# Neighbourhood attention with both heads of a block kept on the two halves of the 128 rows

## The chip, the cores and the metric

The kernel runs on one NeuronCore of a Trainium2 chip. The metric is the device time of one execution in microseconds, as the median of several runs. The engines are TensorE (PE; its weight loads are listed apart as PEld), VectorE (DVE), ScalarE (ACT), GpSimd (POOL) and SyncE (SP, which issues most of the DMAs).

## What is computed

Two layers of a diffusion backbone work on 256 latent tokens and 256 context tokens of width 1024, all in float32. Each layer projects the tokens once; the columns feed a gated linear attention (GLA, 4 heads) and a neighbourhood attention (8 heads of width 64). Both outputs go through one output projection, and a SwiGLU follows (layer 0) or a mixture of 8 experts (layer 1). The part that matters here is the neighbourhood attention. In outline:

```
s_loc = q . k[clamped grid window of the query] + bias        (latent queries)
s_ctx = q . kc                                                (all context keys)
p     = softmax(concat(s_loc, s_ctx))                         (one softmax, float32)
out   = p_loc . v[window] + p_ctx . vc
context queries: softmax(q . kc / sqrt(64)) . vc              (layer 0 only)
```

The kernel computes the scores of a latent query against all 256 latent and 256 context keys at once; keys outside the window get a bias of -1e30.

## The kernel before

**Precision by splitting.** A float32 product on PE is made of products in `float32r`, the rounded type. A tensor x is split in a rounded part r (an ACT copy that writes `float32r`) and a rest l = x - r (a DVE subtraction), and a product of two split tensors is r.r + r.l + l.r (`mm3`, L209 to L212: three matmuls of 128 contraction rows and up to 512 columns).

**Where heads lie.** `nq` and `nk` hold the projected queries and keys transposed: partition = head dimension, so one block b of 128 partitions holds two heads, head 2b on partitions 0 to 63 and head 2b+1 on 64 to 127. `natt` (L936 to L1042) has four blocks.

**`prep(b)` (L941 to L957)** makes the operands of one block. For each of the two heads (j = 0, 1) it builds a tile K2 of 128 partitions with the rounded keys on the head's own half (ACT, L952) and the rest of the keys on the other half (DVE, L954), a tile Q2 with the rounded queries on the own half (ACT, L953) and the queries cast to `float32r` on the other half (DVE, L955), and a tile ql with the rest of the queries on the own half (DVE, L956) and zeros on the other (POOL, L948, once for each pool). So one matmul over 128 rows, Q2 by K2, sums r.r + r.l (L976), and a second, ql by K2, adds l.r (L977). That is two matmuls a head, four for the two heads of a block, all in the full 128 x 128 form, and two ACT and three DVE instructions a head in `prep`, each on 64 partitions.

**One item** is one head of one block for 128 queries, for latent queries (`ctx` = 0, 512 keys) or context queries (`ctx` = 1, 256 keys). Layer 0 has 32 items, 16 of each; layer 1 has 16 items, latent only. Stages of an item: `n1` takes a PSUM bank, runs L976 and L977, adds the bias on DVE (L981), takes the maximum (DVE, L984) and the exponential with its sum (ACT, L987). `n1b` takes the reciprocal (DVE, L993) and scales (DVE, L994). `n2` transposes the probabilities 128 columns at a time (PE, L1004) and copies them out of PSUM (ACT, L1005). `n3`, once for both heads and 256 queries, multiplies by the values (PE, L1019: 128 rows by 64 columns, the two heads on the two column halves), and `na_done` splits the result into HR (ACT, L1077) and HL (DVE, L1078).

**Order.** `run` (L1023) emits `n1` of item i, `n1b` of item i-1, `n2` of item i-3 and `n3` of item i-4, with two yields for an item. `weave(main, filler, each)` (L217) puts steps of other work in after each yield: with `each` a triple (rate, count, later rate), `rate` steps for each of the first `count` yields and `later rate` after. For `natt` the filler is the r projection with its gate (L928 to L930), the transposes of the GLA output (`o_turn`, L1132 to L1137), and, in layer 0, four adaLN column blocks (L356, loads of `w_ada`). `RATE` (L2037) holds the triple of each layer. Within this part a scheduler that builds the program then orders each engine's instructions by priority, which follows the emission, and by when it reckons that their inputs are ready; the engines run them in that fixed order. `prep(0)` is emitted before `natt` starts, at the end of the GLA core; `prep(1)` after the second item; `prep(b+2)` after the last item of block b, since it writes the same buffers. `bias(b)` loads the bias tile of a block through SP (L965, two buffers).

**After it.** The output projection (L622) starts once the last `na_done` is through. In layer 1 it is followed by the router and the experts, whose weights (about 350 MB) are streamed from HBM to the end of the program; the first of their loads are issued with the output projection.

Of the kernel before, what the change touches and what calls it, by code (L numbers as in the profile page):

```python
# [93 lines left out]
def kernel(ctx: ExitStack, tc: tile.TileContext, A: dict, out: bass.AP):  # L94
    nc = tc.nc
# [183 lines left out]
    ident = B_("ident")  # L279
# [656 lines left out]
    def natt(l, full, C, first, nq, nk, nv, done):  # L936


        parts, lows = {}, {}

        def prep(b):  # L941
            pool = na if b % 2 else first[0].pool
            K2 = [pool.tile([P, NT], F32R, tag=f"K2{j}", bufs=1, name=f"K2{j}") for j in range(2)]
            Q2 = [pool.tile([P, nq.shape[2]], F32R, tag=f"Q2{j}", bufs=1, name=f"Q2{j}") for j in range(2)]
            if pool not in lows:
                lows[pool] = [pool.tile([P, nq.shape[2]], F32R, name=f"ql{j}") for j in range(2)]
                for j in range(2):
                    nc.gpsimd.memset(lows[pool][j][64 - 64 * j:P - 64 * j].bitcast(F32), 0.0)  # L948
            ql = lows[pool]
            for j in range(2):  # L950
                own, other = slice(64 * j, 64 * j + 64), slice(64 - 64 * j, P - 64 * j)
# [7 lines left out]
        items = [dict(b=b, ctx=cx, j=j, qt=qt) for b in range(4) for cx in range(2 if full else 1) for j in range(2) for qt in range(2)]  # L959
        Bt, PTs = {}, {}  # L960
        na = None

        def bias(b):
            t = na.tile([P, 2, 6, 64], F32, tag="B", bufs=2, name="B")
            nc.sync.dma_start(t, relD[l][2 * b:2 * b + 2].rearrange("h r q x c -> (r q) h x c"))  # L965
            Bt[b] = t

        def n1(it):
            b, j, qt, cx = it["b"], it["j"], it["qt"], it["ctx"]
            if cx == 0 and j == 1 and qt == 1 and b < 2:  # L970
                bias(b + 2)
            n = 256 if cx else 512
# [5 lines left out]
            if cx == int(full) and j == 1 and qt == 1 and b < 2:  # L978
                prep(b + 2)
            if not cx:  # L980
                nc.vector.tensor_tensor(out=pS[:, 0:256], in0=pS[:, 0:256],  # L981
                                        in1=Bt[b][:, j, 2 - 2 * qt:6 - 2 * qt, :].rearrange("p x c -> p (x c)"), op=ALU.add)
# [5 lines left out]
            it["p"], it["n"], it["rs"] = pr, n, rs  # L988

        def n1b(it):  # L990
            pr, n, rs = it["p"], it["n"], it["rs"]
# [4 lines left out]
        def n2(it):  # L996
            b, j, qt, cx = it["b"], it["j"], it["qt"], it["ctx"]
            nkb = it["n"] // P
            if qt == 0:
                PTs[b, cx, j] = na.tile([P, 4, 256], F32, tag="PT", bufs=3, name="PT")  # L1000
            PT = PTs[b, cx, j]
            pt = ps()
            for i in range(nkb):
                nc.tensor.transpose(pt[:, i * P:(i + 1) * P], it["p"][:, i * P:(i + 1) * P], ident)  # L1004
            nc.scalar.activation(PT[:, :nkb, qt * P:(qt + 1) * P],  # L1005
                                 pt[:, :it["n"]].rearrange("p (a t) -> p a t", a=nkb), AF.Copy)

        def n3(it):

            b, j, qt, cx = it["b"], it["j"], it["qt"], it["ctx"]  # L1010
            if qt == 0 or j == 0:
                return
            kbs = [2, 3] if cx else [0, 1, 2, 3]
            pts = [PTs.pop((b, cx, jj)) for jj in range(2)]
            bank = ps()
            for i, kb in enumerate(kbs):
                for jj in range(2):
                    h = 2 * b + jj
                    nc.tensor.matmul(bank[64 * jj:64 * jj + 64, 0:256], nv[kb][:, h * 64:(h + 1) * 64], pts[jj][:, i, :],  # L1019
                                     start=i == 0, stop=i == len(kbs) - 1)  # L1020
            done(b, cx, bank)

        def run(na_pool):  # L1023
# [1117 lines left out]
```

## Time and profile before

| | |
|---|---|
| median of 3 runs | 1880.4 us (1879.72 to 1882.68) |
| the profiled execution, its own time | 1879.96 us |
| its span, first to last instruction | 1878.1 us |
| mean granted TensorE clock | 0.984 |
| PE, PEld, DVE, ACT, POOL busy | 1797.8, 1297.5, 1189.9, 922.7, 84.2 us |
| neighbourhood attention, layer 0 | about 213 to 300 us from the span's start |
| neighbourhood attention, layer 1 | about 882 to 934 us |

The span is one execution on the chip as the hardware profiler recorded it; the profiled execution's own time is 1.86 us longer than its span. Each engine runs its own queue in order. A wait is listed with the instruction that waited and the one that ended the wait. The busy time of PE counts a matmul until its modelled end; in a stream of matmuls each one starts before the one ahead of it has ended, so the price of a matmul in a stream is the distance between two starts, not the duration in the row.

### The profile page before, as it was taken

What the parts mean: (1) busy time and instruction counts of PE and PEld (TensorE: products, weight loads), DVE (VectorE), ACT (ScalarE), POOL (GpSimd) and SP (SyncE); (2) the same over time, 40 slices, a digit from 0 to 9 for tenths busy, and PEclk for the clock granted to TensorE, in tenths of its full rate; (3) what the DMA queues carried; (4) which work ended last, traced back from release to release, by engine and by line L of the source; (5) the groups of instructions that cost most, each with busy time, mean ns of one, the idle gap of its engine ahead of it and who ended that gap; (6) DMA issues with size and microseconds to landing.
All of it is one profiled execution on the core that took longest, in us unless ns stands there. A gap on an engine that the chain in (4) does not pass through costs nothing. (4 is left out here: it accounts for less than half of the span.)

```text
span 1878.1 us, 25461 instructions
## 1 busy us (share of the span) xinstructions
PE 1797.8 (96%) x8773; PEld 1297.5 (69%) x8773; DVE 1189.9 (63%) x1750; ACT 922.7 (49%) x1329; POOL 84.2 (4%) x103
## 2 busy tenths in 40 slices
PE   5999899999999998999899999999999999999995
PEld 3688566877788887787577853588886358888731
DVE  4457686478642345368879951599996249999701
ACT  3443376522222336443757831577774247777501
POOL 2100200110000002001000000000000000000000
PEclk8999999999999999999899999999999999999998
DMA  9432546267763332424299999999999999999996
GB/s 327 137 105 52 183 163 221 79 197 255 227 190 92 121 109 66 141 79 130 58 341 340 325 347 404 409 409 404 409 378 350 407 406 408 404 409 385 340 408 262
DMA packets 203321, 491.90 MB, mean 262 GB/s; under 512 B 29744, under 2 KB 71248, under 8 KB 203184
## 3 DMA queue, kind: packets, MB, share of 16 engines
q1 hardware_dynamic: 201152, 483.12, 71.0%
q0 software_dynamic: 2032, 7.08, 1.1%
q8 instruction: 71, 1.16, 0.3%
q14 instruction: 66, 0.54, 0.1%
HBM read 485.94 MB, written 4.98 MB: 261 GB/s over the span
## 5 line engine op out<-in xcount | busy, mean ns | idle before, releaser
L170 DVE TENSOR_TENSOR wl<-raw,wr 128x1024 fp32r<-128x1024 f32 x446 | 536.1, 1225 | 132.9 <-ACT wr L169 128.7
L169 ACT ACTIVATE wr<-raw 128x1024 fp32r<-128x1024 f32 x446 | 465.8, 1059 | 295.3 <-PE ps L211 152.0
L210 PE MATMUL ps<-wr,HR 128*128 128x512 f32 x736 | 299.3, 407 | 2.5 <-ACT wr L169 2.5
L211 PE MATMUL ps<-wl,HR 128*128 128x512 f32 x736 | 294.4, 400 | 7.5 <-DVE wl L170 6.5
L212 PE MATMUL ps<-wr,HL 128*128 128x512 f32 x736 | 292.3, 397 | 0.0
L210 PE MATMUL ps<-HR,wr 128*128 128x512 f32 (+1 forms) x592 | 220.3, 373 | 9.6 <-ACT HR L1979 6.2
L211 PE MATMUL ps<-HL,wr 128*128 128x512 f32 (+1 forms) x592 | 218.5, 369 | 3.4 <-POOL HL L521 1.7
L212 PE MATMUL ps<-HR,wl 128*128 128x512 f32 (+1 forms) x592 | 217.4, 367 | 0.5 <-DVE wl L170 0.5
L211 PEld LDWEIGHTS ps<-wl,HR 128*128 128x128 f32 x736 | 139.5, 190 | 47.0 <-DVE wl L170 14.7
L210 PEld LDWEIGHTS ps<-wr,HR 128*128 128x128 f32 x736 | 139.5, 190 | 40.5 <-issue 4.7
L212 PEld LDWEIGHTS ps<-wr,HL 128*128 128x128 f32 x736 | 139.2, 189 | 32.5
L210 PEld LDWEIGHTS ps<-HR,wr 128*128 128x128 f32 x592 | 111.6, 189 | 41.8 <-issue 8.6
L211 PEld LDWEIGHTS ps<-HL,wr 128*128 128x128 f32 x592 | 112.3, 190 | 23.6 <-DVE HL L1984 3.4
L212 PEld LDWEIGHTS ps<-HR,wl 128*128 128x128 f32 x592 | 112.4, 190 | 19.2 <-DVE wl L170 1.0
L1600 PE MATMUL ps<-raw,xw 128*64 128x512 f32 (+1 forms) x596 | 117.2, 536 | 2.2 <-DMA raw<-in_moe_w_gate 1.1
L1615 DVE TENSOR_TENSOR hid<-hid,ps 128x512 f32<-128x512 f32 (+1 forms) x47 | 31.3, 665 | 132.9 <-PE ps L1600 132.9
L210 PE MATMUL ps<-wr,tr 128*128 128x512 f32 x280 | 111.9, 400 | 0.0
L211 PE MATMUL ps<-wl,tr 128*128 128x512 f32 x280 | 110.6, 395 | 0.0
L212 PE MATMUL ps<-wr,tl 128*128 128x512 f32 x280 | 110.4, 394 | 0.0
L1600 PEld LDWEIGHTS ps<-raw,xw 128*64 128x64 f32 x596 | 40.7, 137 | 66.4 <-issue 53.3
L405 DVE SCALAR_TENSOR_TENSOR sums<-raw,condS,sums 128x512 f32<-128x512 f32 x98 | 71.6, 761 | 19.6 <-DMA raw<-in_w_ada 18.8
L1600 PE MATMUL ps<-raw,tw 128*64 128x512 f32 x272 | 67.2, 605 | 3.9 <-DMA raw<-in_moe_w_down 2.8
(368 smaller groups left out, 2433.6 us busy)
## 6 DMA issues: line engine op xcount, KB each, us to landing
raw<-in_moe_w_down SPq DMA_DIRECT2D x180, 512.0 KB
raw<-in_moe_w_gate SPq DMA_DIRECT2D x169, 512.0 KB
raw<-in_moe_w_up SPq DMA_DIRECT2D x167, 512.0 KB
raw<-in_w_ada SPq DMA_DIRECT2D x80, 512.0 KB
raw<-in_w_in SPq DMA_DIRECT2D x48, 512.0 KB
HR1w<-in_moe_w_up SPq DMA_DIRECT2D x24, 512.0 KB
raw<-in_ffn_w_gate SPq DMA_DIRECT2D x22, 512.0 KB
raw<-in_ffn_w_up SPq DMA_DIRECT2D x22, 512.0 KB
```

Source lines behind the costliest of these rows:

```text
L169: nc.scalar.activation(wr, raw, AF.Copy)
L170: nc.vector.tensor_tensor(out=wl, in0=raw, in1=wr.bitcast(F32), op=ALU.subtract)
L210: nc.tensor.matmul(o, lr, rr, start=start, stop=False)
L211: nc.tensor.matmul(o, lr, rl, start=False, stop=False)
L212: nc.tensor.matmul(o, ll, rr, start=False, stop=stop)
L405: nc.vector.scalar_tensor_tensor(out=o, in0=i_, scalar=s_, in1=o, op0=ALU.mult, op1=ALU.add)
L1600: nc.tensor.matmul(o[a * HALF:(a + 1) * HALF, 0:n], x, raw[:, a * n:(a + 1) * n], start=start, stop=stop)
L1615: nc.vector.tensor_tensor(out=hid, in0=hid, in1=st.pop((fb, 1))[:, 0:w], op=ALU.mult)
```

## The change

A block's two heads stay where the projection put them. `prep(b)` splits the whole 128-partition block at once, keys and queries: one ACT copy and one DVE subtraction for each. An item is now both heads of a block for 128 queries. Its scores are three products for each head (r.r, r.l, l.r) of 64 contraction rows, head 0 on rows 0 to 63 and head 1 on rows 64 to 127, in turns, each head into a PSUM bank of its own. The zeroed halves (L948) and the cast (L955) are gone. `n1`, `n1b`, `n2` become `scores`, `soft`, `scaled`, `turned`, the last three once a head; an item's `turned` and `n3` come one item (two heads) later instead of three and four heads later, with four yields to an item. Layer 1's triple changes from (.65, 40, .65) to (1, 11, .5). The load of the next bias tile is emitted after the last use of its buffer instead of ahead of it.

```diff
         def prep(b):
             pool = na if b % 2 else first[0].pool
-            K2 = [pool.tile([P, NT], F32R, tag=f"K2{j}", bufs=1, name=f"K2{j}") for j in range(2)]
-            Q2 = [pool.tile([P, nq.shape[2]], F32R, tag=f"Q2{j}", bufs=1, name=f"Q2{j}") for j in range(2)]
-            if pool not in lows:
-                lows[pool] = [pool.tile([P, nq.shape[2]], F32R, name=f"ql{j}") for j in range(2)]
-                for j in range(2):
-                    nc.gpsimd.memset(lows[pool][j][64 - 64 * j:P - 64 * j].bitcast(F32), 0.0)
-            ql = lows[pool]
-            for j in range(2):
-                own, other = slice(64 * j, 64 * j + 64), slice(64 - 64 * j, P - 64 * j)
-                nc.scalar.activation(K2[j][own], nk[own, b, :], AF.Copy)
-                nc.scalar.activation(Q2[j][own], nq[own, b, :], AF.Copy)
-                nc.vector.tensor_tensor(out=K2[j][other], in0=nk[own, b, :], in1=K2[j][own].bitcast(F32), op=ALU.subtract)
-                nc.vector.tensor_copy(Q2[j][other], nq[own, b, :])
-                nc.vector.tensor_tensor(out=ql[j][own], in0=nq[own, b, :], in1=Q2[j][own].bitcast(F32), op=ALU.subtract)
-            parts[b] = K2, Q2, ql
+            parts[b] = []
+            for nm, t in (("k", nk), ("q", nq)):
+                hi, lo = (pool.tile([P, t.shape[2]], F32R, tag=nm + x, bufs=1, name=nm + x) for x in "rl")
+                nc.scalar.activation(hi, t[:, b, :], AF.Copy)
+                nc.vector.tensor_tensor(out=lo, in0=t[:, b, :], in1=hi.bitcast(F32), op=ALU.subtract)
+                parts[b] += [hi, lo]
...
-        def n1(it):
...
-            pS = ps()
-            K2, Q2, ql = parts[b]
+        def scores(it):
+            b, qt, cx = it["b"], it["qt"], it["ctx"]
+            n = it["n"] = 256 if cx else 512
+            it["s"] = [ps() for _ in range(2)]
+            kr, kl, qr, ql = parts[b]
             tok = slice(cx * 256 + qt * P, cx * 256 + (qt + 1) * P)
-            nc.tensor.matmul(pS[:, :n], Q2[j][:, tok], K2[j][:, NT - n:NT], start=True, stop=False)
-            nc.tensor.matmul(pS[:, :n], ql[j][:, tok], K2[j][:, NT - n:NT], start=False, stop=True)
+            for i, (q, k) in enumerate(((qr, kr), (qr, kl), (ql, kr))):
+                for j in range(2):
+                    nc.tensor.matmul(it["s"][j][:, :n], q[half[j], tok], k[half[j], NT - n:NT], start=i == 0, stop=i == 2)
...
-            for i in range(n + 4):
-                if i < n:
-                    n1(items[i])
-                if i == 1:
+            for i in range(n + 1):
+                it, old = (items[i] if i < n else None), (items[i - 1] if i else None)
+                if it:
+                    scores(it)
+                    soft(it, 0)
+                if i == 0:
                     prep(1)
                 yield
-                if 0 <= i - 1 < n:
-                    n1b(items[i - 1])
-                if 0 <= i - 3 < n:
-                    n2(items[i - 3])
-                if 0 <= i - 4 < n:
-                    n3(items[i - 4])
+                if it:
+                    soft(it, 1)
+                    if it["ctx"] == 0 and it["qt"] == 1 and it["b"] < 2:
+                        bias(it["b"] + 2)
+                if old:
+                    turned(old, 0)
+                yield
+                if it:
+                    scaled(it, 0)
+                if old:
+                    turned(old, 1)
+                yield
+                if it:
+                    scaled(it, 1)
+                if old:
+                    n3(old)
                 yield
...
-    RATE, FILL = ((1.2, 17, .5), (.65, 40, .65)), (5, 6)
+    RATE, FILL = ((1.2, 17, .5), (1, 11, .5)), (5, 6)
```

## Rows read from the trace of the kernel before

**Rows 1.** Busy by stage: length, PE, PEld, DVE, ACT, POOL, clock, DMA, GB/s.
```profile
213.00:300.00 87.00, 79.04 (x467) 51.67 (x468) 70.38 (x172) 57.50 (x135) 8.72 (x9) 0.98 0.66 220
882.00:934.00 52.00, 42.66 (x217) 30.23 (x218) 45.42 (x107) 35.04 (x75) 1.64 (x3) 0.87 0.29 94
1100.00:1864.00 764.00, 751.88 (x3420) 488.58 (x3420) 485.65 (x498) 415.20 (x475) 2.34 (x3) 1.00 1.00 391
```

**Rows 2.** The same view in stretches of 10 us, inside layer 1's stage.
```profile
890.00:900.00 10.00, 6.33 (x21) 4.60 (x20) 9.72 (x23) 5.33 (x11) 0.00 (x0) 0.66 0.26 73
```

**Rows 3.** Waits of PE in layer 1's stage, 882 to 934: total, times, longest us.
```profile
PE ps L1004 <- DVE p L994: 8.0, 6, 3.7
```

**Rows 4.** Waits of PE in layer 0's stage, 213 to 300.
```profile
PE ps L211 <- DVE wl L170: 3.6, 1, 3.6
PE ps L1004 <- DVE p L994: 3.4, 4, 1.3
```

**Rows 5.** DVE groups by line, 882 to 934: busy us, mean ns, idle before.
```profile
L954 DVE TENSOR_TENSOR K<-nk,K 64x512 fp32r<-64x512 f32 x6 | 4.1, 685 | 0.2
L955 DVE CAST Q<-nq 64x256 fp32r<-64x256 f32 x6 | 3.0, 499 | 0.2
...
L956 DVE TENSOR_TENSOR ql<-nq,Q 64x256 fp32r<-64x256 f32 x6 | 2.5, 417 | 0.1
...
L365 DVE TENSOR_TENSOR adarows<-ps,adarows 128x512 fp32r<-128x512 f32 x1 | 0.7, 693 | 0.0
```

**Rows 6.** DVE groups by line, 213 to 300.
```profile
L954 DVE TENSOR_TENSOR K<-nk,K 64x512 fp32r<-64x512 f32 x6 | 4.3, 714 | 0.2
L956 DVE TENSOR_TENSOR ql<-nq,Q 64x512 fp32r<-64x512 f32 x6 | 4.1, 685 | 0.1
...
L955 DVE CAST Q<-nq 64x512 fp32r<-64x512 f32 x6 | 2.5, 419 | 0.1
```

**Rows 7.** ACT groups by line, 882 to 934.
```profile
L952 ACT ACTIVATE K<-nk 64x512 fp32r<-64x512 f32 x6 | 3.7, 622 | 0.1
...
L953 ACT ACTIVATE Q<-nq 64x256 fp32r<-64x256 f32 x6 | 2.4, 406 | 2.1 <-PE ps L976 2.1
```

**Rows 8.** Timeline of PE around an expert's scatter: start us, us, instruction, count.
```profile
1196.71 0.39 PE L211 MATMUL ps<-wl,HR 128*128 128x512 f32 x1
1196.94 0.40 PE L212 MATMUL ps<-wr,HL 128*128 128x512 f32 x1
1197.27 0.51 PE L1733 MATMUL ps<-yr,GT 64*128 64x512 f32 x2
1197.60 0.41 PE L1734 MATMUL ps<-yl,GT 64*128 64x512 f32 x2
1197.83 0.41 PE L1733 MATMUL ps<-yr,GT 64*128 64x512 f32 x2
1198.07 0.40 PE L1734 MATMUL ps<-yl,GT 64*128 64x512 f32 x2
1198.40 0.50 PE L210 MATMUL ps<-wr,HR 128*128 128x512 f32 x1
1198.74 0.40 PE L211 MATMUL ps<-wl,HR 128*128 128x512 f32 x1
```

**Rows 9.** Timeline of PE at an item of 256 keys in layer 0.
```profile
245.56 0.28 PE L976 MATMUL ps<-K,Q 128*128 128x256 f32 x1
...
245.68 0.28 PE L977 MATMUL ps<-K,ql 128*128 128x256 f32 x1
...
245.79 0.40 PE L210 MATMUL ps<-wr,HR 128*128 128x512 f32 x1
```

**Rows 10.** Waits of SP's queue, 882 to 934.
```profile
SPq L965 <- DVE ps L981: 10.2, 1, 10.2
```

**Rows 11.** Timeline of the end of layer 1's stage.
```profile
929.33 0.48 DVE L994 TENSOR_SCALAR p<-p,ri 128x512 f32<-128x512 f32 x1
...
930.58 3.89 PE L1019 MATMUL ps<-PT,nv 128*64 128x256 f32 x16
...
934.40 0.73 PE L622 MATMUL psh<-wr,HR 128*128 128x512 f32 x2
```

More of the change, by code (lines that the diff above doesn't have):

```diff
@@ L936, in natt @@
     def natt(l, full, C, first, nq, nk, nv, done):
-        parts, lows = {}, {}
+        parts = {}
+        half = [slice(0, 64), slice(64, P)]
         def prep(b):
             pool = na if b % 2 else first[0].pool
-            K2 = [pool.tile([P, NT], F32R, tag=f"K2{j}", bufs=1, name=f"K2{j}") for j in range(2)]
-            Q2 = [pool.tile([P, nq.shape[2]], F32R, tag=f"Q2{j}", bufs=1, name=f"Q2{j}") for j in range(2)]
-            if pool not in lows:
-                lows[pool] = [pool.tile([P, nq.shape[2]], F32R, name=f"ql{j}") for j in range(2)]
-                for j in range(2):
-                    nc.gpsimd.memset(lows[pool][j][64 - 64 * j:P - 64 * j].bitcast(F32), 0.0)
-            ql = lows[pool]
-            for j in range(2):
-                own, other = slice(64 * j, 64 * j + 64), slice(64 - 64 * j, P - 64 * j)
-                nc.scalar.activation(K2[j][own], nk[own, b, :], AF.Copy)
-                nc.scalar.activation(Q2[j][own], nq[own, b, :], AF.Copy)
-                nc.vector.tensor_tensor(out=K2[j][other], in0=nk[own, b, :], in1=K2[j][own].bitcast(F32), op=ALU.subtract)
-                nc.vector.tensor_copy(Q2[j][other], nq[own, b, :])
-                nc.vector.tensor_tensor(out=ql[j][own], in0=nq[own, b, :], in1=Q2[j][own].bitcast(F32), op=ALU.subtract)
-            parts[b] = K2, Q2, ql
-        items = [dict(b=b, ctx=cx, j=j, qt=qt) for b in range(4) for cx in range(2 if full else 1) for j in range(2) for qt in range(2)]
+            parts[b] = []
[4 more added lines that the diff above has]
+                parts[b] += [hi, lo]
+        items = [dict(b=b, ctx=cx, qt=qt) for b in range(4) for cx in range(2 if full else 1) for qt in range(2)]
         Bt, PTs = {}, {}
@@ L966, in bias, with soft @@
             Bt[b] = t
-        def n1(it):
[L969 to L972, printed above, removed]
-            pS = ps()
-            K2, Q2, ql = parts[b]
+        def scores(it):
[3 more added lines that the diff above has]
+            kr, kl, qr, ql = parts[b]
             tok = slice(cx * 256 + qt * P, cx * 256 + (qt + 1) * P)
-            nc.tensor.matmul(pS[:, :n], Q2[j][:, tok], K2[j][:, NT - n:NT], start=True, stop=False)
-            nc.tensor.matmul(pS[:, :n], ql[j][:, tok], K2[j][:, NT - n:NT], start=False, stop=True)
-            if cx == int(full) and j == 1 and qt == 1 and b < 2:
+            for i, (q, k) in enumerate(((qr, kr), (qr, kl), (ql, kr))):
+                for j in range(2):
+                    nc.tensor.matmul(it["s"][j][:, :n], q[half[j], tok], k[half[j], NT - n:NT], start=i == 0, stop=i == 2)
+            if cx == int(full) and qt == 1 and b < 2:
                 prep(b + 2)
-            if not cx:
+            it["p"], it["rs"] = [None] * 2, [None] * 2
+        def soft(it, j):
+            n, pS, qt = it["n"], it["s"][j], it["qt"]
+            if not it["ctx"]:
                 nc.vector.tensor_tensor(out=pS[:, 0:256], in0=pS[:, 0:256],
-                                        in1=Bt[b][:, j, 2 - 2 * qt:6 - 2 * qt, :].rearrange("p x c -> p (x c)"), op=ALU.add)
+                                        in1=Bt[it["b"]][:, j, 2 - 2 * qt:6 - 2 * qt, :].rearrange("p x c -> p (x c)"), op=ALU.add)
             nm = na.tile([P, 1], F32, tag="nm", bufs=5, name="nm")
@@ L987, in n1, with scaled @@
             nc.scalar.activation(pr[:, :n], pS[:, :n], AF.Exp, bias=nm, accum_out=rs)
-            it["p"], it["n"], it["rs"] = pr, n, rs
-        def n1b(it):
-            pr, n, rs = it["p"], it["n"], it["rs"]
+            it["p"][j], it["rs"][j] = pr, rs
+        def scaled(it, j):
+            pr, n, rs = it["p"][j], it["n"], it["rs"][j]
             ri = na.tile([P, 1], F32, tag="ri", bufs=5, name="ri")
@@ L994, in n1b, with turned @@
             nc.vector.tensor_scalar(out=pr[:, :n], in0=pr[:, :n], scalar1=ri, scalar2=None, op0=ALU.mult)
-        def n2(it):
-            b, j, qt, cx = it["b"], it["j"], it["qt"], it["ctx"]
+        def turned(it, j):
+            b, qt, cx = it["b"], it["qt"], it["ctx"]
             nkb = it["n"] // P
@@ L1003, in n2 @@
             for i in range(nkb):
-                nc.tensor.transpose(pt[:, i * P:(i + 1) * P], it["p"][:, i * P:(i + 1) * P], ident)
+                nc.tensor.transpose(pt[:, i * P:(i + 1) * P], it["p"][j][:, i * P:(i + 1) * P], ident)
             nc.scalar.activation(PT[:, :nkb, qt * P:(qt + 1) * P],
@@ L1008, in n3 @@
         def n3(it):
-            b, j, qt, cx = it["b"], it["j"], it["qt"], it["ctx"]
-            if qt == 0 or j == 0:
+            b, qt, cx = it["b"], it["qt"], it["ctx"]
+            if qt == 0:
                 return
```

## Prediction, made before the changed kernel ran

> **What bounds the kernel now.** I read the busy time by stage first, to see which engine has no room where the change acts. In layer 1's attention stage DVE is busy 45.42 of 52 us while PE is idle 9.3 us [rows 1]. Inside it DVE fills 9.72 of 10 us, and there PE's granted clock is 0.66 of full, so part of that stretch ran at 1.2 instead of 2.4 GHz, after PE had been idle for over a third of it [rows 2]. Then the waits: PE's largest one is for probabilities that DVE has still to scale, 8.0 us [rows 3]. So layer 1's stage hangs on DVE. In layer 0's stage PE is busy 79.04 of 87 us [rows 1]; of the idle 8 us, 3.6 are one wait for a weight split, which the change doesn't touch, and 3.4 are waits for scaled probabilities [rows 4]. That stage is PE's, with some help to be had from DVE. What comes behind counts too: from 1100 us on, DMA share and PE are both full [rows 1], with a stream of weights that starts with the output projection of layer 1. A stage that ends earlier starts the stream earlier, and I pass its gain to the end one to one; the same for layer 0, behind which PE works without a break.
>
> **DVE in `prep`, layer 1.** Six halves of `prep` lie in the stage (both heads of b = 1, 2, 3; block 0 is done before it): 4.1 + 3.0 + 2.5 = 9.6 us [rows 5]. In their place stand three keys splits and three queries splits over 128 partitions. The subtraction of 128x512 takes 693 ns and that of 64x512 685 ns [rows 5], so the partitions cost nothing and the columns count: 3 x (0.69 + 0.42) = 3.3 us. DVE saves 9.6 - 3.3 = 6.3 us, on the engine that bounds. The rest of its work (bias, maximum, reciprocal, scale) keeps its count and shapes.
>
> **DVE in `prep`, layer 0.** Here 4.3 + 4.1 + 2.5 = 10.9 us go [rows 6] and 6 x 0.69 = 4.1 come: 6.8 us less on an engine that is not the bound. It can shorten PE's waits for probabilities, 3.4 us at most [rows 4].
>
> **ACT and POOL.** ACT's copies halve: in layer 1 3.7 + 2.4 = 6.1 us [rows 7] become 3 x (0.62 + 0.41) = 3.1. ACT is busy 35.04 of 52 us [rows 1], so I count nothing; its cover is DVE's longer work, and if ACT became the bound these 3 us would be a gain, not a cost. Block 0's `prep` and POOL's clearing of ql lie under the GLA core, beside PE; nothing.
>
> **Scores on PE: the two halves.** No row shows scores on 64 rows, but an expert's scatter has 64-row matmuls of 512 columns on both halves, each half into its own bank [rows 8]. Each line there holds two matmuls in 0.40 to 0.51 us, where one alone takes 0.39 to 0.50, and the next pair starts 0.23 or 0.24 us later: 0.23 is also the step of single 128-row matmuls in the same rows (1196.71 to 1196.94). Two half matmuls cost one slot. An item of two heads took four slots and will take three: -0.23 us for 512 keys. With 256 keys a slot is 245.68 - 245.56 = 0.12 us [rows 9]; no row has half matmuls that short, so a pair lies between 0.12 (as for 512) and 0.24 (not side by side). I take 0.12, as the loads of the pairs in rows 8 hide like those of single ones: -0.12 us.
>
> **Scores on PE: the change of form.** In the same rows the step from the 128-row stream to the 64-row one is 0.33, the next one 0.33, and on the way back 0.33 and 0.34 [rows 8], where 0.23 would follow in either stream. A change of form costs 0.20 us, there and back 0.41. Today's scores have the form of the transposes and projections around them; the changed ones never do. So an item pays +0.41 - 0.23 = +0.18 us with 512 keys and +0.41 - 0.12 = +0.29 with 256. Layer 0 (8 + 8 items): 1.4 + 2.3 = +3.7 us. Layer 1 (8 items): +1.4 us. Lower end: where an item stands next to `n3`, which has a third form already, one of the two changes is there today; for all 24 items that takes 4.8 us off. Upper end: the scheduler puts other matmuls between the three products, and each break costs another 0.41. I take one unbroken group an item, since all six need only tiles that `prep` left ready long before, except for the first block.
>
> The Trainium skill has a rule that speaks against this change: by "TensorEngine Tiling (Array Packing)", Key Properties, going to another tiling mode drains the array. It gives no price; "TensorE: Matmul & The Clock Gate", Single matmul latency, puts the part of an isolated matmul that a stream hides at about 166 ns at the full clock. An estimate from these two would be 0.17 us a change in place of 0.20, thus 24 x 0.07 = 1.6 us less over both layers; the rows decide, and the sum goes by 0.20.
>
> **Order.** An item's transposes now follow one item behind its scores instead of three heads, so the lag in which softmax must finish shrinks from 1.5 items to one: 52 / 8 = 6.5 us in layer 1 and 87 / 16 = 5.4 in layer 0. I count no new wait, because DVE has less in its queue; without that cover the price is in the second rival. Layer 1's new triple is done with the ten steps of the r projection at yield 10, after 2.5 of 8 items, where 10 / 0.65 = 15.4 yields, or 7.7 of 16 heads, were needed: the same filler, on PE's idle 9.3 us, earlier. The bias load that moves behind its buffer's last reader waits in SP's queue for that reader today already (10.2 us) [rows 10]; behind it are loads of the output weights, at a DMA share of 0.29 [rows 1]: nothing. Four yields an item in layer 0 are two a head as before.
>
> **The end of the stage.** From the last scaling at 929.33 to the output projection at 934.40 [rows 11] five us pass that no saving in `prep` shortens. That the last two heads now go together could take something off, or add the wait of one for the other; at most the 3.89 us of the value product, which would be some 2 at full clock, so 2 us either way. I take nothing.
>
> **The sum.** Layer 1: -6.3 on DVE; PE has 9.3 us idle, of which 3.0 would be left, and 1.4 more to do in a chain that DVE and PE share by turns, so I give that back in full: -4.9. Layer 0: +3.7 on PE, less the 3.4 us of waits that shorter DVE queues can give back: +0.3. Together -4.6 us. The profiled execution took 1879.96 us and would take 1875.4; it lies 0.4 below the median of 1880.4, so for a median I forecast 1875.8.
>
> **The rivals.** (1) *PE's changes of form decide (slower).* Were the three products of each item torn apart twice, 24 x 2 x 0.41 = 19.7 us more of PE would come: 13.1 in layer 0, where nothing hides them, and 6.6 in layer 1, of which about 2 fit in what is idle. That gives 1875.8 + 13.1 + 4.6 = 1893.5. It turns the sign from about 11 breaks in layer 0 on (4.6 / 0.41). For it: the first block's operands come just in time, and other matmuls are always at hand. Against it: after the first block the operands lie ready two blocks ahead. With half as many breaks it is 1884.7. Chance 0.14. (2) *The shorter lag takes it back.* PE meets a transpose whose probabilities aren't scaled, as it does for 8.0 us now [rows 3], and DVE's saving turns into PE's waiting: layer 1 gains 1 to 2 us, layer 0 pays 0 to 1: 1879. For it: that wait is the largest already, and the lag is a third shorter. Against it: DVE's queue is what made it. Chance 0.24. (3) *Layer 0 gains as well.* Where the changes of form fall beside `n3` and the 32-column adaLN matmuls, most of the 3.7 us is shared, and the 3.4 us of waits go: another -3, and a PE without gaps in layer 1 keeps its full clock [rows 2], another -1.5: 1871.3. Chance 0.20. (4) *The halves don't run side by side.* Each item then takes three slots more than counted: 16 x 0.69 + 8 x 0.36 = 13.9 us, 1889.7 if all of it lands. Rows 8 speak plainly against it. Chance 0.02. The forecast keeps 0.40.
>
> By the Trainium skill, "TensorEngine Tiling (Array Packing)", Theoretical Speedup, two tiles give up to twice the rate; rival (4) is where that would fail, and rows 8 show the full factor for 512 columns.
>
> **How the numbers follow.** A measurement of this kernel tells 0.2% from no change, 3.8 us, so faster means under 1876.6 and slower over 1884.2. The forecast's own range is 1873 to 1879: the terms shared with `n3` below, 2 us of the stage's end either way and waits of layer 0 that stay above. About two thirds of it lie under 1876.6, all of (3) does, and some of (2): 0.51. Slower are (4) and most of (1): 0.14. The rest, 0.35, is within. To leave out no more than 2 in 10 the range takes in (3) and (2) and stops within (1): 1869.5 to 1883.
>
> **What would show it.** In the changed kernel's profile: no cast and half the `prep` instructions; scores in pairs that start together, 0.23 us apart, with steps of about 0.33 before and after each group of six; layer 1's stage some 5 us shorter, with DVE under 41 us busy and fewer waits for its scaling; layer 0's stage as long as now. It is wrong if groups of 64-row matmuls come singly, if layer 0's stage is over 3 us longer, or if PE's waits at the transposes are as long as before though DVE has idle time.

## The result, and the profile after

The changed kernel took **1891.06 us** (median of 5 runs, 1889.33 to 1896.65), the kernel before 1881.74 beside it: a ratio of **1.0057, interval 1.0044 to 1.0071**. The forecast was 1875.8 in a range of 1869.5 to 1883.0, so the sign and the range were both wrong. The profiled execution took 1889.33 us with a span of 1887.6; that of before had a span of 1878.1. The 9.5 us between them are what the traces have to explain.

A stage goes here from the first matmul of L481 (a broadcast of gate rows that stands just ahead of the attention items) to the first output projection (L622). Busy time by stage, columns as in [rows 1]: first the kernel before, with these ends, layer 0 above layer 1.

```profile
211.25:300.42 89.17, 81.20 (x473) 52.26 (x473) 72.42 (x181) 58.57 (x139) 8.72 (x9) 0.98 0.66 221
882.00:934.40 52.40, 43.06 (x219) 30.24 (x219) 45.42 (x107) 35.04 (x75) 1.82 (x4) 0.87 0.29 93
```

The same view of the changed kernel:

```profile
209.40:308.20 98.80, 84.45 (x504) 51.14 (x504) 67.22 (x170) 55.39 (x135) 8.16 (x9) 0.97 0.61 205
888.30:940.20 51.90, 43.36 (x234) 26.94 (x234) 40.58 (x95) 31.25 (x69) 2.15 (x4) 0.93 0.30 94
```

Layer 0's stage is 9.6 us longer although DVE and ACT have less to do and PE only 3.3 us more: 14 of its 99 us PE stands idle, where it was 8 of 89. Layer 1's stage is as long as before although DVE is busy 4.8 us less. The rest of the 9.5: layer 0's stage starts 1.9 us earlier (between profiles its start scatters from 209.4 to 213.1), the work between the stages takes 1.5 less, that behind layer 1 3.7 more.

PE's waits in layer 0's stage of the changed kernel (waiting line, what ended it, total us, times, longest):

```profile
PE ps L211 <- DVE wl L170: 4.2, 2, 3.2
PE ps L999 <- DVE p L989: 2.1, 2, 1.2
PE ps L1014 <- ACT PT L1000: 2.0, 4, 1.3
...
PE ps L999 <- DVE sc L457: 1.8, 1, 1.8
PE ps L999 <- DVE ri L988: 1.4, 2, 1.3
PE ps L999 <- ACT HR L1143: 1.0, 1, 1.0
```

The transposes (L999) and the value product (L1014) wait 8.3 us in all, where the transposes waited 3.4 [rows 4].

So time is lost in waiting. The same waits in layer 1's stage, which answer to the 8.0 us of [rows 3]:

```profile
PE ps L999 <- DVE p L989: 3.1, 3, 2.2
PE ps L999 <- ACT p L982: 2.6, 1, 2.6
PE ps L999 <- DVE ri L988: 1.6, 1, 1.6
```

Three names, one meaning: a transpose (L999) stands ready for probabilities that are in the exponential, the reciprocal or the scaling. 7.3 us, while DVE is idle for 11. What DVE waits for in layer 0's stage, the three longest:

```profile
DVE HL L1085 <- ACT HR L1084: 11.8, 6, 4.3
DVE r L929 <- ACT r L928: 8.8, 4, 3.4
DVE gtb L483 <- DMA bb<-in_b_ada: 3.0, 1, 3.0
```

The first is new in size: 2.0 us in the kernel before. In layer 1 it is 5.7 us. DVE stands at the split of a value product's result (`na_done`). The timeline shows how this goes. PE near the end of layer 1's stage (start us, us, instruction, count, idle time before it):

```profile
928.55 0.80 PE L968 MATMUL ps<-kr,qr 64*128 64x512 f32 x2
929.28 3.12 PE L1014 MATMUL ps<-PT,nv 128*64 128x256 f32 x14
932.32 0.49 PE L968 MATMUL ps<-kl,qr 64*128 64x512 f32 x2
932.66 0.40 PE L968 MATMUL ps<-kr,ql 64*128 64x512 f32 x2
...
936.26 1.39 PE L999 MATMUL ps<-cst_base,p 128*128 128x128 f32 x8 [2.19 <-DVE p L989]
937.60 2.67 PE L1014 MATMUL ps<-PT,nv 128*64 128x256 f32 x16
```

DVE beside it:

```profile
932.85 0.42 DVE L1085 TENSOR_TENSOR HL<-ps,HR 128x256 fp32r<-128x256 f32 x1 [2.78 <-ACT HR L1084]
933.19 0.75 DVE L976 TENSOR_TENSOR ps<-ps,B 128x256 f32<-128x256 f32 x2
933.85 1.28 DVE L979 TENSOR_REDUCE nm<-ps 128x1 f32<-128x512 f32 x2
935.52 0.16 DVE L988 RECIPROCAL ri<-rs 128x1 f32<-128x1 f32 x1 [0.39 <-ACT p L982]
935.72 0.49 DVE L989 TENSOR_SCALAR p<-p,ri 128x512 f32<-128x512 f32 x1
```

The first score products of the last item run at 928.55, then 14 of the 16 matmuls of the previous block's value product, and only at 932.32 the other two pairs. DVE meanwhile waits 2.8 us for that value product; behind its split stand the item's bias, maximum, reciprocal and scaling. When they have run, PE has waited 2.2 us at the transposes. One item is in flight and PE and DVE work by turns. The same tear stands one item earlier (918.2 to 922.0), and at layer 0's last item (299.25 to 301.43).

### The profile page after: what moved, and what is told of

Same layout as the page of the kernel before. It is cut to its first block, busy times and chain, and to the rows that moved or that the text cites. A ratio compares the mean times of both kernels' runs of the same rounds, so it can differ in the third digit from the quotient of the medians.

```text
span 1887.6 us, 25473 instructions
## 1 busy us (share of the span) xinstructions
PE 1803.3 (96%) x8821; PEld 1295.8 (69%) x8821; DVE 1176.1 (62%) x1718; ACT 912.7 (48%) x1313; POOL 81.0 (4%) x95
```

## The experiments

Each row is one kernel beside the kernel before on the same chip. "New order" stands for the order of the change with one item of lag; "old order" for three heads of lag and the value product one head later still. The stages' ends are rounded to 0.1 us, and each stage is that of one profile: e1, e9 and e10, whose times are alike, lie 0.9 us apart in layer 0 and 0.5 in layer 1.

| kernel | median us | ratio to before, interval | stage L0 | stage L1 |
|---|---|---|---|---|
| before (medians; stages of its profile) | 1879 to 1882 | 1 | 89.2 | 52.4 |
| the change | 1891.06 | 1.0057 [1.0044, 1.0071] | 98.8 | 51.9 |
| e1 new products, old order | 1874.90 | 0.9963 [0.9951, 0.9976] | 88.9 | 43.2 |
| e2 old products, new order | 1904.28 | 1.0123 [1.0106, 1.0140] | 103.7 | 60.3 |
| e3 change, lag two items | 1880.15 | 0.9994 [0.9983, 1.0005] | 92.5 | 46.6 |
| e4 change, old triple | 1889.65 | 1.0050 [1.0033, 1.0067] | 98.6 | 51.0 |
| e5 change, scores urgent | 1885.26 | 1.0026 [1.0016, 1.0035] | 98.6 | 47.5 |
| e6 = e1 + DVE work | 1878.59 | 0.9982 [0.9973, 0.9992] | 89.4 | 49.4 |
| e7 = e3 + e5 | 1876.54 | 0.9977 [0.9966, 0.9987] | 90.7 | 46.6 |
| e8 before, lag two heads | 1898.61 | 1.0093 [1.0076, 1.0109] | 102.8 | 55.8 |
| e9 = e1, scores urgent | 1872.58 | 0.9960 [0.9946, 0.9974] | 88.8 | 43.5 |
| e10 = e1, head after head | 1872.53 | 0.9967 [0.9956, 0.9979] | 89.8 | 43.0 |
| e11 = e1, lag four heads | 1869.18 | 0.9945 [0.9930, 0.9960] | 87.3 | 42.2 |
| e12 = e1, lag five heads | 1870.59 | 0.9945 [0.9930, 0.9959] | 88.6 | 42.5 |
| e13 = e1, new triple | 1875.36 | 0.9973 [0.9963, 0.9983] | 88.8 | 45.6 |
| e14 change, values later | 1878.67 | 0.9992 [0.9983, 1.0002] | 92.9 | 45.1 |
| e15 = e14 + e3 | 1871.88 | 0.9961 [0.9947, 0.9975] | 87.4 | 43.3 |
| e16 before, transposes sooner | 1895.27 | 1.0081 [1.0064, 1.0098] | 99.4 | 54.9 |

**Products or order: e1 and e2.** The change has two halves that can be had alone. e1 keeps the new `prep` and the 64-row products and puts them into the old loop:

```diff
-            for i in range(n + 1):
-                it, old = (items[i] if i < n else None), (items[i - 1] if i else None)
...
+            for i in range(n + 4):
+                if i < n:
+                    n1(items[i])
...
+                if 0 <= i - 3 < n:
+                    n2(items[i - 3])
+                if 0 <= i - 4 < n:
+                    n3(items[i - 4])
```

> The new products and the new prep, in the order of the kernel before: heads one after the other, the six products with the first head of a pair, transposes three heads behind, n3 four heads behind, old triple in layer 1. Theory F (the change of TensorE's form costs): the loss stays, 1887 to 1892 us. Theory O (the new order costs: transposes only one item behind the scores, so the softmax chain lies open): the loss goes and the saving on DVE shows, 1875 to 1880 us, layer 1's stage about 47 us.

One thing in e1 is not as before: a block's two heads for the same queries follow each other, and their six products come with the first, so the scores of every second head lie one head further ahead.

e2 keeps the new loop and puts back the old `prep` and the two full-height products a head:

```diff
-            for i, (q, k) in enumerate(((qr, kr), (qr, kl), (ql, kr))):
-                for j in range(2):
-                    nc.tensor.matmul(it["s"][j][:, :n], q[half[j], tok], k[half[j], NT - n:NT], start=i == 0, stop=i == 2)
+            for j in range(2):
+                nc.tensor.matmul(it["s"][j][:, :n], Q2[j][:, tok], K2[j][:, NT - n:NT], start=True, stop=False)
+                nc.tensor.matmul(it["s"][j][:, :n], ql[j][:, tok], K2[j][:, NT - n:NT], start=False, stop=True)
```

> The old prep and the old two full-height products a head, in the new order with the new triple. Theory F: the loss goes, 1879 to 1883 us. Theory O: it stays or grows, since DVE has its old work as well, 1889 to 1896 us.

The four corners agree. By the ratios, as shares of 1881.9 us, the products are worth 0.37% or -7.0 us in the old order and 1.0123 - 1.0057 = 0.66% or -12.4 in the new one; the order costs 1.0057 - 0.9963 = 0.94% or +17.7 with the new products and +23 with the old ones. The products do what was forecast and more, though some of the 7.0 us may belong to the further lead of every second head in e1; the order takes it back more than once.

**What DVE's saving is worth: e6.** To e1, three subtractions of 128x512 are added to each `prep` of blocks 1 to 3, into a tile that nobody reads.

```diff
+            if b:
+                void = na.tile([P, NT], F32, tag="void", bufs=1, name="void")
+                for _ in range(3):
+                    nc.vector.tensor_tensor(out=void, in0=nk[:, b, :], in1=parts[b][0].bitcast(F32), op=ALU.subtract)
```

> The kernel with the new products in the old order (1874.9, layer 1's stage 43.2 us), with three more subtractions of 128x512 on DVE in each preparation of blocks 1 to 3, into a tile that nobody reads: 3 x 0.69 = 2.1 us a block, 6.2 us a layer, which is what the new preparation saves DVE. Theory (layer 1's stage gains what DVE saves): layer 1's stage goes to 48 to 50 us, layer 0's grows by under 1, time 1880 to 1882. Rival (layer 1 gains by the three products on half the rows, DVE's saving is beside the path): layer 1's stage 43 to 45 us, 1875 to 1877.

Layer 1's stage in e1, then in e6:

```profile
881.90:925.10 43.20, 38.82 (x234) 25.27 (x234) 39.17 (x95) 31.24 (x69) 2.68 (x4) 1.00 0.35 113
```

```profile
879.70:929.10 49.40, 40.19 (x234) 25.60 (x234) 44.28 (x104) 31.99 (x69) 2.68 (x4) 0.97 0.30 99
```

Nine subtractions, 6.1 us by their durations and 5.1 by the busy time (their rows overlap those of their neighbours), make the stage 6.2 us longer; layer 0's grows by 0.5. PE's wait for scaled probabilities, 3.9 us in e1's layer 1 and 8.0 before, is here:

```profile
PE ps L1003 <- DVE p L993: 8.3, 9, 1.7
```

The stage came as the theory said, the time did not: 1878.6 instead of 1880 to 1882, because only about 4 of the 6 us reach the end of the program (below).

**Lag and torn groups: e3, e5, e7.** e3 lets the transposes and the value product follow two items behind the scores instead of one, with six buffers of probabilities instead of four; e5 gives the six score products priority over other matmuls that are ready; e7 does both.

```diff
...
-            for i in range(n + 1):
-                it, old = (items[i] if i < n else None), (items[i - 1] if i else None)
+            for i in range(n + 2):
+                it, old = (items[i] if i < n else None), (items[i - 2] if i > 1 else None)
```

```diff
+        @urgent
         def scores(it):
```

> The changed kernel with transposes and n3 two items behind the scores instead of one (six probability buffers instead of four). Theory F: no gain, 1889 to 1893 us. Theory O: most of the loss goes, 1877 to 1883 us, and PE's waits for probabilities shrink in both stages.

> The changed kernel with the six products of an item emitted at high priority, so that n3 is not put between them. If the torn groups are what costs (in layer 1 the last item's second and third products start 3.8 us after the first), 1884 to 1887 us; if the lag alone costs, 1889 to 1893 us as the changed kernel.

> The changed kernel with both edits: transposes two items behind their scores, and the six score products ahead of other matmuls that are ready. Theory (lag and torn groups are the whole price of the order, 16 us, and the two are partly the same wait): better than either alone, layer 0's stage 90 to 92 us and layer 1's 43.5 to 45.5, time 1875 to 1878. Rival (the two edits mend the same wait, the late scores): no better than the lag alone, 1880, layer 1's stage 46.6. Rival (early scores only fill DVE's queue): worse than the lag alone, over 1881.

The lag alone gives back 6.3 us in layer 0 and 5.3 in layer 1; urgent scores nothing in layer 0 and 4.4 in layer 1, where two of the three late tears were. Together they come within 1.8 and 3.4 us of e1. In e5 DVE's waits for the value product in layer 0 fall from 11.8 to 2.7 us, but 11.3 us of waits for scores stand in their place and the stage is as long as before: a mended wait says little while the chain stays.

**The triple: e4 and e13.** e4 puts (.65, 40, .65) back into the change. In this kernel the last steps of the r projection are emitted after block 0's value product, which writes its result over rows of HR that these steps read, so they compute with other data and wait for that write; its time bounds the triple's share only roughly.

> The changed kernel with layer 1's old triple (0.65 of a filler step a yield) in place of the new one. Theory (the order costs by its shorter lag and by value products that come between the score products; the triple only moves the filler): layer 0's stage stays at 98.8 us; in layer 1 the r projection then lasts 15 of 26 yields instead of 10, so PE has work while it waits for probabilities, and the stage shortens by 1 to 3 us: 1888 to 1890. Rival (the triple is the larger part of what layer 1 loses by the new order, since its filler is gone by a third of the stage): layer 1's stage falls from 51.9 to about 45 us and the time to about 1884. If the filler's place is worth nothing: 1891.

Layer 1's stage is 0.9 us shorter, so the rival fell, as far as this kernel can tell. The earlier r projection isn't a free choice either: with the value product that early, it must be through by then. e13 tries the new triple in the old order.

```diff
-    RATE, FILL = ((1.2, 17, .5), (.65, 40, .65)), (5, 6)
+    RATE, FILL = ((1.2, 17, .5), (1, 11, .5)), (5, 6)
```

> The kernel with the new products in the old order (1874.9, layer 1's stage 43.2 us), with the new triple in layer 1: the r projection's ten steps at one a yield instead of 0.65. Theory (the triple only moves filler, and at three heads of lag there is little to fill): layer 1's stage 43 to 44.5, 1874.5 to 1876.5. Rival (the filler is missed later in the stage, and this is what is left of layer 1's loss when lag and torn groups are mended, 46.6 against 43.2): 46 to 48, 1877.5 to 1880.

The stage grows by 2.4 us, between the two expectations; of this about 2 us show in the ratios (0.9973 against 0.9963, with overlapping intervals). In this order the triple seems to have a small price of its own; e15 below, with the same triple and no price in layer 1 (43.3 us), shows that it isn't a fixed one.

**Is it the lag? e8, e14, e15, e16.** e8 shortens the lag of the kernel before to two heads, transposes and value product alike.

```diff
...
-                if 0 <= i - 3 < n:
-                    n2(items[i - 3])
-                if 0 <= i - 4 < n:
-                    n3(items[i - 4])
+                if 0 <= i - 2 < n:
+                    n2(items[i - 2])
+                if 0 <= i - 3 < n:
+                    n3(items[i - 3])
```

> The kernel before, with its transposes two heads behind their scores instead of three, everything else as it was. Theory (layer 0 and layer 1 need the lag, whatever the products are): layer 0's stage 2 to 5 us longer than 89.1, layer 1's 1 to 4 longer than 52.4: 1885 to 1890. Rival (two heads would do; what costs is the order inside an item, not the lag): 1882, both stages within 1 us of the kernel before.

It costs 17.5 us, far more than I had expected, 13.6 of it in layer 0: without any of the new products, the old kernel loses by lag alone what the change loses by its order. That looked like the whole answer. e14 tested it: the change with its lag of one item, but the value product two yields later, behind the next item's scores, bias and maxima.

```diff
...
                 if it:
                     soft(it, 1)
...
+                if i > 1:
+                    n3(items[i - 2])
                 if old:
                     turned(old, 0)
...
-                if old:
-                    n3(old)
```

> The changed kernel with the value product of a pair of items emitted two yields later: behind the next item's scores, bias additions and maxima, ahead of its own item's transposes. The transposes keep their lag of one item. Theory (the transposes come too soon after their scores, whatever stands around them): layer 0's stage stays at 96 to 99 us and layer 1's at 50 to 53: 1888 to 1892. Rival (the lag itself is enough; DVE is held in its queue by the split of the value product's result, 11.8 us of waits in layer 0, with the next item's bias and maxima behind it): those waits fall under 4 us, layer 0's stage to 91 to 95, layer 1's to 46 to 49, time 1879 to 1884.

My theory fell. With the lag unchanged, 12 of the 17.7 us come back (1.0057 - 0.9992). DVE's wait for the value product in layer 0's stage of e14, against the 11.8 us above:

```profile
DVE HL L1085 <- ACT HR L1084: 2.5, 2, 1.3
```

DVE's wait for the r projection's gate (L929 for L928) grows from 8.8 to 13.4 us in the same stage, which is 5.9 us shorter all the same. Only groups at the start of each stage are still torn, and layer 1's granted clock is 1.00. The edit moves the product on PE and its split on DVE together and doesn't part the two; e5, which mends the torn groups on PE alone, gives back 5.8 us (1.0057 - 1.0026). So both moved parts had to be tried again apart: e15 adds e3's lag to e14, e16 moves only the transposes of the kernel before and leaves its value product four heads behind (of e8's edit, the first half).

> The changed kernel with both: transposes two items behind their scores, and the value product two yields later, behind the next item's bias and maxima. Theory (two separate prices, the value product's place and the transposes' lag; in layer 1 the triple's own 2.4 us stay): layer 0's stage 88 to 90.5, layer 1's 43 to 45, time 1873 to 1876. Rival (both edits mend one and the same wait): no better than the later value product alone, stages 92 to 93 and 45, 1878 to 1880.

> The kernel before with its transposes two heads behind their scores instead of three, but with its value product where it was, four heads behind. Theory (what cost 17.5 us with both moved is the transposes' lag): layer 0's stage 97 to 103, time 1892 to 1899. Rival (it is the value product's place in DVE's queue there too): layer 0's stage 89 to 93, time 1881 to 1887.

Stages of e14, then of e15, then of e16, layer 0 above layer 1:

```profile
210.00:302.90 92.90, 81.64 (x504) 49.73 (x504) 66.25 (x170) 54.69 (x135) 7.98 (x9) 0.96 0.64 214
883.50:928.60 45.10, 39.04 (x234) 25.18 (x234) 40.02 (x95) 31.44 (x69) 2.25 (x4) 1.00 0.33 108
```

```profile
209.70:297.10 87.40, 79.89 (x504) 49.64 (x504) 65.10 (x169) 53.37 (x133) 8.49 (x9) 0.98 0.67 231
879.20:922.50 43.30, 39.34 (x235) 25.68 (x235) 39.24 (x95) 30.89 (x69) 1.96 (x3) 1.00 0.35 111
```

```profile
211.60:311.00 99.40, 84.27 (x473) 53.26 (x473) 74.15 (x182) 60.37 (x141) 8.74 (x9) 0.95 0.61 204
890.70:945.60 54.90, 40.41 (x219) 28.44 (x219) 46.73 (x107) 35.40 (x75) 1.82 (x4) 0.91 0.28 89
```

e15 is as fast as e1, with the items, yields and triple of the new order: lag and place of the value product together are the whole price against e1, and their shares overlap (12 us each alone, 18 together). Its lag is four heads, though; against e11 below, which has that lag in the old order, 0.16% are left, with overlapping intervals. e16 shows that on the kernel before the lag of the transposes costs nearly all of e8's loss. Where its time goes, DVE's longest waits in layer 0's stage of e16:

```profile
DVE nm L984 <- PE ps L977: 5.4, 6, 1.9
DVE ps L981 <- PE ps L977: 5.1, 6, 2.6
DVE HL L1078 <- ACT HR L1077: 4.2, 3, 2.6
```

Before, the same three were 1.5, 3.4 and 2.0. DVE waits for scores that stand behind transposes on PE, which wait for DVE (6.2 us for scaled probabilities, 3.4 before): the turns again.

**How much lag: e11 and e12.** e1 with one and two heads more of lag, and as many more buffers of probabilities.

```diff
...
-                if 0 <= i - 3 < n:
-                    n2(items[i - 3])
-                if 0 <= i - 4 < n:
-                    n3(items[i - 4])
+                if 0 <= i - 4 < n:
+                    n2(items[i - 4])
+                if 0 <= i - 5 < n:
+                    n3(items[i - 5])
```

> The kernel with the new products in the old order, with the transposes four heads behind instead of three (five buffers of probabilities instead of four). Theory (the lag is what hides softmax; at three heads 3.9 us of waits for scaled probabilities are left in layer 1): layer 1's stage 41 to 43 us, layer 0's 88 to 89: 1872 to 1875. Rival (three heads are enough, and one more only makes the stage's end longer, when nothing is left to cover the last softmax): layer 1's stage 44 to 46, 1876 to 1878.

> As with four heads of lag (1869.2, stages 87.3 and 42.2 us), with the transposes five heads behind their scores (six buffers of probabilities). Theory (the lag only covers the waits for softmax, and with four heads 2.9 us of them are left in layer 1 and about none in layer 0): layer 0's stage 86.5 to 88, layer 1's 41 to 42.5, time 1867 to 1870. Rival (a longer lag also lengthens the stage's end, where no score covers the last softmax and transposes): layer 1's stage 43 to 45, 1870 to 1873.

In these profiles the fourth head takes 1.6 us off layer 0's stage and 1.0 off layer 1's. The times give 0.18% against e1, with overlapping intervals, so the gain is likely and not shown. The fifth head brings nothing. **e11 has the lowest median found: 1869.18 us, 0.9945**, faster than the kernel before and the changed one; by its ratio it can't be told from e12.

**Smaller questions: e9 and e10.** e9 gives e1's scores priority, as e5 does. e10 issues an item's six products head after head instead of by turns:

```diff
-                for i, (q, k) in enumerate(((qr, kr), (qr, kl), (ql, kr))):
-                    for jj in range(2):
+                for jj in range(2):
+                    for i, (q, k) in enumerate(((qr, kr), (qr, kl), (ql, kr))):
```

> The kernel with the new products in the old order, with the six score products ahead of other matmuls that are ready. Theory (with transposes three heads behind, softmax has its time and scores need not be early): only the first item of each layer is torn there, so both stages stay within 1 us of 88.9 and 43.2: 1874 to 1876. Rival (earlier scores take 2 us or more off PE's waits for scaled probabilities, 3.9 us in layer 1): 1870 to 1873.

> The kernel with the new products in the old order (1874.9), but an item's six score products head after head: three on rows 0 to 63 into one bank, then three on rows 64 to 127 into the other, instead of by turns. Theory (the halves run side by side only because neighbours in the stream lie on different halves): six slots instead of three an item, 8 x 0.69 + 8 x 0.36 = 8.4 us more of PE in layer 0 and 8 x 0.69 = 5.5 in layer 1, where some 3 of it fit into PE's waits: layer 0's stage 95 to 98 us, layer 1's 44 to 47, time 1882 to 1888. Rival (a half runs beside whatever is next on the other half, within a wider stretch, so that turns don't matter): 1875, both stages within 1 us.

Neither differs from e1: with lag enough, urgent scores have nothing to mend, and the turns in which the change issues the products don't matter. One item on PE in e10, where the queue holds three products of one head and then three of the other:

```profile
267.43 0.51 PE L971 MATMUL ps<-kr,qr 64*128 64x512 f32 x2
267.77 0.40 PE L971 MATMUL ps<-kl,qr 64*128 64x512 f32 x2
268.00 0.40 PE L971 MATMUL ps<-kr,ql 64*128 64x512 f32 x2
268.33 1.05 PE L356 MATMUL ps<-raw,condS 128*32 128x512 f32 x5
```

The two heads' products still run beside each other, and the next matmul starts 0.90 us after the first; in e1 that is 267.50 to 268.39, 0.89. The two starts of a pair lie 10 ns apart in e10 and 2 to 4 in e1. My theory of neighbours in the stream was wrong.

## Why the prediction was wrong

**The step that failed is *Order***: "I count no new wait, because DVE has less in its queue; without that cover the price is in the second rival." Its lag was worked out right (6.5 and 5.4 us instead of 1.5 times that), but it was never held against the chain that has to fit in. That chain could be read from the profile of before: an item's bias, maximum, exponential, reciprocal and scaling for two heads, with the value product of the pair before it on PE and its split on DVE, emitted between them. An estimate from its rows in layer 1, if nothing overlaps: 3.5 us on DVE for the two heads (0.42 + 0.68 + 0.16 + 0.48 each), 0.9 for an exponential with its sum, 1.95 for a value product at full clock and 0.8 for its split, some 7 us. I looked for what DVE has in its queue, not for which instruction it stops at: the step moved `n3` next to the following item's softmax, and the split of `n3`'s result is ahead of that softmax on DVE. By e3, e14 and e15 lag and place cost 18 us together.

**The second rival** had the right mechanism, and its price was the mistake: "layer 0 pays 0 to 1". Layer 0 paid 9.6. I took its stage for PE's because PE was busy for 79 of 87 us [rows 1], and waits of 3.4 us [rows 4] for a measure of what softmax could cost. They only showed what is left with three heads of lag; e16 shows the price with two, 10.2 us in layer 0. The range was cut inside the first rival by the same error, and that rival has the wrong mechanism: there were six breaks in 24 groups where it counted 48, and the three late ones were the value product's. Urgent scores, without a torn group, still lose 0.26%.

**The assumption "one unbroken group an item"** failed in those six places. The two late breaks in layer 1 held an item's scores back by 3.8 us each; mended alone (e5) the stage gives back 4.4. The late one in layer 0 held them 2.2 us.

**What held.** *DVE in `prep`, layer 1*: 6.3 us off were counted; busy time falls by 6.25, from 45.42 to 39.17 in e1, and e6 shows that the stage follows DVE's work. The closeness is part luck: `prep`'s own rows fall by 5.3, from 9.6 to 4.3, and the other 0.9 is small differences and overlaps elsewhere. The mean of 499 ns for a cast [rows 5] holds one of 1.56 us beside an instruction of POOL, where the others take 0.29, and in e1 a subtraction is held the same way (last section); without the two 8.3 us would go and 3.3 come. *Layer 0's `prep`*: 7.1 us less on DVE in e1 for 6.8 counted, and the stage is 0.3 us shorter, with +0.3 forecast. *ACT and POOL*: ACT is busy 3.8 us less in e1's layer 1; what that is worth by itself no run shows. *The end of the stage*: from the start of the last scaling to the output projection 3.8 us to its first matmul, 4.8 to its second, instead of 5.1 [rows 11], inside the 2 us allowed.

*The two halves and the change of form* were priced right. A 512-key item in the changed kernel's stream of 128-row matmuls:

```profile
902.27 0.39 PE L211 MATMUL ps<-wl,HR 128*128 128x512 f32 x1
902.50 0.40 PE L212 MATMUL ps<-wr,HL 128*128 128x512 f32 x1
902.83 0.50 PE L968 MATMUL ps<-kr,qr 64*128 64x512 f32 x2
903.16 0.39 PE L968 MATMUL ps<-kl,qr 64*128 64x512 f32 x2
903.39 0.40 PE L968 MATMUL ps<-kr,ql 64*128 64x512 f32 x2
903.72 0.50 PE L210 MATMUL ps<-wr,HR 128*128 128x512 f32 x1
904.06 0.40 PE L211 MATMUL ps<-wl,HR 128*128 128x512 f32 x1
```

The steps are 0.33, 0.33, 0.23, 0.33 and 0.34 where 0.23 would stand: 0.40 a visit, for the 0.41 of the forecast, and a pair is one slot. For 256 keys, which no row of before showed, a pair of e1 steps on by 262.44 - 262.32 = 0.12, the lower of the two bounds. By the Trainium skill, "TensorEngine Tiling (Array Packing)", Key Properties, changing the tiling mode drains the array; the trace agrees, at that 0.40 there and back.

***The sum* was too small for layer 1**: -4.9 for what e1 shows as -9.2. Of the 9.2, e6 puts some 6 to DVE. The 1.4 us of PE that I charged "in full" were not paid: PE's granted clock over the stage is 1.00 instead of 0.87, after waits for scaled probabilities of 3.9 us, the longest 1.7, instead of 8.0 and 3.7, and its busy time falls from 43.06 to 38.82 us although it has more matmuls. The third rival had this effect at 1.5 us. No run tries the clock by itself.

**"I pass its gain to the end one to one"** holds only roughly. Layer 1's output projection starts 9.3 us earlier in e1 and the span is 4.9 shorter; in e11 13.3 and 11.5; in the changed kernel 5.8 us later and 9.5 longer. Part of it goes in the router and first expert, where the granted clock of the second 20 us from the start of the output projection differs from run to run (0.84 in the kernel before, 0.74 in e1, 0.73 after the change, 0.80 in e11). The clock doesn't explain it: in e10 and e15 it is 0.75 there, and from that start to the end of the program they take 944.2 and 943.2 us, as the kernel before with 943.7, where e1 takes 948.1; e9, with 0.84, takes 948.0. The cause stays open, and one profile tells little here: e1's executions alone lie between 1870.63 and 1876.24 us.

## What to carry to other kernels

A software pipeline's lag is part of its price list: before shortening it, add up the chain from the first instruction that fills a buffer to the one that needs it, on all engines, and compare it with the new lag; the waits that the profile showed at the old lag (3.4 us) said nothing of the price at a shorter one (10.2). On an engine that runs in order, look at what is emitted between two steps of that chain: here the split of a finished product stood ahead of the next softmax, and moving the emission of product and split by two yields was worth 12 us. Change products and order in separate steps, as the one here was worth -7 us and the other +18.

## What the runs showed of the hardware

Products on the two halves of the rows run side by side whether the queue holds them by turns or head after head (0.89 and 0.90 us for six). By the Trainium skill, "TensorEngine Tiling (Array Packing)", Key Properties, tiles work independently of each other; the trace agrees.

A DVE instruction that runs beside one of POOL can be held. In the changed kernel, POOL's multiplication first, then the three DVE instructions around it:

```profile
891.66 1.67 POOL L484 TENSOR_TENSOR gtb<-gtb,gb 128x512 f32<-128x512 f32 x1 [15.17 <-DVE gtb L483]
```

```profile
890.90 0.68 DVE L483 TENSOR_TENSOR gtb<-ps,bb 128x512 f32<-128x512 f32 x1
891.50 0.68 DVE L948 TENSOR_TENSOR kl<-nk,kr 128x512 fp32r<-128x512 f32 x1
892.10 1.52 DVE L948 TENSOR_TENSOR ql<-nq,qr 128x256 fp32r<-128x256 f32 x1
```

The subtraction of 128x256 takes 1.52 us there, where the other two of the stage take 0.41; it ends 0.29 us after POOL's. The subtraction ahead of it runs beside POOL for half a microsecond and takes its usual 0.68. In e1 the one beside POOL is a 128x512 with 1.78 instead of 0.67. In the kernel before it is a cast, 1.56 instead of 0.29. Bias additions, which read PSUM, take their usual 0.42 beside the same line of POOL (224.47 us in the changed kernel). A mean over a line hides a held one: 0.78 for the three subtractions of 128x256.
